# Reordering the transfers of an RMSNorm kernel and choosing the moment at which its stores are queued

## The chip, the cores and the metric

The kernel runs on one core of one Trainium2 chip. The metric is the device time of one execution in microseconds (us). The span in a profile is about 1.8 us shorter than the time (160.9 us against 162.69 us for the profiled run of the kernel before).

## The reference

```python
x: [16, 1024, 512] float32, gamma: ones(512), eps: 1e-5

def reference(x, gamma, eps):
    rms = np.sqrt(np.mean(x ** 2, axis=-1, keepdims=True) + eps)
    x_norm = x / rms * gamma
    return np.maximum(x_norm, 0).astype(np.float32)
```

That is 16,384 rows of 512 numbers: 33.55 MB in, 33.55 MB out, and very little arithmetic on each number.

## The kernel before

The rows are cut into eight chunks of 4 MB (128 partitions, 16 rows on each). There are six slots in SBUF, the on-chip memory, so chunks 6 and 7 reuse the slots of chunks 0 and 1. ACT (ScalarE) squares and sums, then takes the root; DVE (VectorE) multiplies by the reciprocal and gamma and clips at zero, in place. Both work in groups of eight rows, two groups to a chunk, sixteen in all. Every large transfer is issued from SP (SyncE) and so stands in one queue. This is the part that the change touches:

```python
    def store(i):
        nc.sync.dma_start(out=ov[i], in_=slot_ap(i)).then_inc(sem_slot[i % nslots], 16)
    ...
        for m, (i, a, r) in enumerate(loads):       # chunk 0 in two halves
            if i < nslots:
                load(m)
        nxt = nslots
        for i in range(nchunks):
            nc.sync.wait_ge(done, per * (i + 1))     # DVE has finished chunk i
            store(i)
            if i >= 1 and nxt < nchunks:
                nc.sync.wait_ge(sem_slot[nxt % nslots], 32)   # that slot's store has landed
                for m, (c, a, r) in enumerate(loads):
                    if c == nxt:
                        load(m)
                nxt += 1
    ...
        with nc.vector.Fori(0, ngroups) as gi:       # DVE, one group of eight rows
            ...
            for j in range(G):
                row = slots[:, bass.ds(base + j * d, d)]
                r = nc.vector.scalar_tensor_tensor(
                    out=row, in0=row, scalar=rstd[:, bass.ds(col + j, 1)], in1=gamma_sb,
                    op0=ALU.mult, op1=ALU.mult)
                if j == G - 1:
                    r.then_inc(sv, 1)
            ...
            nc.vector.tensor_scalar_max(out=blk, in0=blk, scalar1=0.0).then_inc(done, 1)
```

With L for a load, S for a store and the digit for the chunk, the queue holds L0 to L5, S0, S1, L6, S2, L7, S3 to S7.

## Time and profile before

| what | before | where it is read |
|---|---|---|
| time | 162.76 us, median of 3 (162.70 to 162.78) | timed runs |
| first packet starts, last ends | 1.96 us, 159.39 us | packet records of the trace |
| one transfer of 4 MB, first packet to the next one's first packet | 9.68 us, L5 alone 10.26 us | the same |
| DVE's last instruction ends | 146.43 us | timeline |

I call the time from a transfer's first packet to the first packet of the next a *stage*. If the queue never runs dry, the stages add up to the length of the stream, and the kernel's time is that length plus a fixed start and end. So the way to read this kernel is to list its stages and look for those that are longer than 9.68 us. I call such an excess a *lump*.

### The profile page before, as it was taken

How to read it: one execution, taken by the hardware profiler on the slowest of the kernel's cores; microseconds unless marked ns; L12 is line 12 of the kernel's file. 1: busy time of each engine (PE TensorE's matmuls, PEld its weight loads, DVE VectorE, ACT ScalarE, POOL GpSimd, SP SyncE). 2: the span in 40 equal slices, each digit the busy share in tenths (PEclk: the TensorE clock that was granted, in tenths of full speed). 3: DMA queues.
4: the chain of work that ended last, by engine and by line, in shares of the span. 5: the costliest groups of instructions: out<-in, count | busy, mean ns of one | idle time of the engine just before them, and what ended most of it. 6: DMA issues, size and time to landing. Idle time of an engine off the chain costs nothing. (4 is left out here: it accounts for less than half of the span.)

```text
span 160.9 us, 1006 instructions
## 1 busy us (share of the span) xinstructions
DVE 126.0 (78%) x164; ACT 86.3 (54%) x273; POOL 0.2 (0%) x4
## 2 busy tenths in 40 slices
DVE  1103989898989899999999999999999999994000
ACT  3088929889988988988900198503994000000000
POOL 0000000000000000000000000000000000000000
DMA  5999999999999998999999999999999999999993
GB/s 155 434 432 415 521 391 391 513 399 391 489 424 391 481 432 367 415 391 489 424 391 489 424 391 448 464 391 440 456 407 432 456 415 424 464 415 424 464 407 138
DMA packets 2456, 67.12 MB, mean 417 GB/s; under 512 B 276, under 2 KB 276, under 8 KB 280
## 3 DMA queue, kind: packets, MB, share of 16 engines
q1 hardware_dynamic: 2448, 67.11, 97.6%
q10 hardware_dynamic: 8, 0.01, 0.0%
HBM read 33.56 MB, written 33.55 MB: 417 GB/s over the span
## 5 line engine op out<-in xcount | busy, mean ns | idle before, releaser
L124 ACT ACTIVATE junk<-slots 128x512 f32 x128 | 74.5, 582 | 30.6 <-ACTq L120 30.3
L148 DVE SCALAR_TENSOR_TENSOR slots<-slots,rstd,gamma_sb 128x512 f32 x128 | 86.2, 747 | 4.8 <-DVEq L145 4.8
L155 DVE TENSOR_SCALAR slots<-slots x16 | 36.7, 2294 | 2.4 <-DVEq L154 0.2
L124 ACT ACTIVATION_READ_ACCUMULATOR junk<-slots x128 | 23.9, 187 | 0.0
L142 DVE RECIPROCAL rstd<-rms x16 | 3.1, 196 | 6.3 <-DVEq L138 6.3
L131 ACT ACTIVATE rms<-ss,eps_sb x16 | 4.8, 301 | 3.0 <-ACTq L130 3.0
L135 DVE LOAD_MASK_SELECT gamma_sb<-gseed x1 | 0.0, 14 | 5.8 <-DMA gseed<-in_gamma_dram 5.8
L116 ACT ACT_TABLE_LOAD x1 | 1.3, 1283 | 2.8 <-issue 2.8
L109 DVE MEMSET gseed<- 128x512 f32 x1 | 0.5, 485 | 1.1 <-SPq L90 1.1
L135 DVE STREAM_SHUFFLE gamma_sb<-gseed 128x512 f32<-128x512 f32 x1 | 0.7, 715 | 0.0
L180 POOL MEMSET const-bfloat16-1.0<- 128x1 bf16 x1 | 0.1, 103 | 0.0
L180 POOL MEMSET const-uint8-127<- 128x1 uint8 x1 | 0.1, 102 | 0.0
L180 POOL MEMSET const-float32-0.0<- 128x1 f32 x1 | 0.1, 100 | 0.2 <-issue 0.2
L180 POOL MEMSET const-float32-1.0<- 128x1 f32 x1 | 0.1, 99 | 0.0
L110 DVE MEMSET eps_sb<- 128x1 f32 x1 | 0.1, 59 | 0.0
## 6 DMA issues: line engine op xcount, KB each, us to landing
out_dram<-slots SPq DMA_DIRECT2D x8, 4096.0 KB, 31.3
slots<-in_x_dram SPq DMA_DIRECT2D x7, 4096.0 KB, 30.3
slots<-in_x_dram SPq DMA_DIRECT2D x2, 2048.0 KB, 9.6
gseed<-in_gamma_dram ACTq DMA_DIRECT2D x1, 8.0 KB
```

What stands on the lines that cost most here:

```text
L109: nc.vector.memset(gseed, 0.0).then_inc(sem_z, 1)
L110: nc.vector.memset(eps_sb, eps).then_inc(sem_z, 1)
L116: nc.scalar.preload_act_table(ACTF.Sqrt)
L124: a = nc.scalar.activation(out=junk[:, j, :], in_=slots[:, bass.ds(base + j * d, d)], func=ACTF.Square, accum_out=ss[:, bass.ds(col + j, 1)])
L131: nc.scalar.activation(out=rms[:, bass.ds(col, G)], in_=ss[:, bass.ds(col, G)], func=ACTF.Sqrt, bias=eps_sb, scale=inv_d).then_inc(sq, 1)
L135: nc.vector.stream_shuffle(gamma_sb, gseed, [0] * 32)
L142: nc.vector.reciprocal(out=rstd[:, bass.ds(col, G)], in_=rms[:, bass.ds(col, G)]).then_inc(sv, 1)
L148: r = nc.vector.scalar_tensor_tensor(out=row, in0=row, scalar=rstd[:, bass.ds(col + j, 1)], in1=gamma_sb, op0=ALU.mult, op1=ALU.mult)
L155: nc.vector.tensor_scalar_max(out=blk, in0=blk, scalar1=0.0).then_inc(done, 1)
L180: nc = _bacc.Bacc("TRN2", target_bir_lowering=False, num_devices=1)
```

## The change

L6 and L7 now stand together, which leaves two places where a store stands behind a load instead of three: S0 behind L5 and S2 behind L7. At both, SP holds the store back until DVE reaches a chosen row, so that it enters the queue when the last packets of that load are under way. The intent is to shorten the stream at these places. The stores' data are ready long before; no wait of another kind is removed.

```diff
     def store(i):
+        nc.sync.wait_ge(done, per * (i + 1))
         nc.sync.dma_start(out=ov[i], in_=slot_ap(i)).then_inc(sem_slot[i % nslots], 16)
...
-        nxt = nslots
-        for i in range(nchunks):
-            nc.sync.wait_ge(done, per * (i + 1))
+        nc.sync.wait_ge(tick3, 6)
+        store(0)
+        store(1)
+        for s in range(2):
+            nc.sync.wait_ge(sem_slot[s], 32)
+            load(7 + s)
+        nc.sync.wait_ge(tick1, 11)
+        for i in range(2, nchunks):
             store(i)
-            if i >= 1 and nxt < nchunks:
-                nc.sync.wait_ge(sem_slot[nxt % nslots], 32)
-                for m, (c, a, r) in enumerate(loads):
-                    if c == nxt:
-                        load(m)
-                nxt += 1
...
+                if j == 0:
+                    r.then_inc(tick1, 1)
+                if j == 2:
+                    r.then_inc(tick3, 1)
                 if j == G - 1:
                     r.then_inc(sv, 1)
```

(`load(7)` and `load(8)` are chunks 6 and 7, since chunk 0 has two loads.)

More of the change, by code (lines that the diff above doesn't have):

```diff
@@ L64 @@
     sq = tc.alloc_semaphore("sq")
+    tick1 = tc.alloc_semaphore("tick1")
+    tick3 = tc.alloc_semaphore("tick3")
     done = tc.alloc_semaphore("done")
```

## The prediction

> **What bounds the kernel now.** I read the page's DMA rows first, then the waits of the SP queue, then the busy time stage by stage, then the timelines of SP and of DVE. The page:
>
> ```profile
> span 160.9 us, 1006 instructions
> DVE 126.0 (78%) x164; ACT 86.3 (54%) x273; POOL 0.2 (0%) x4
> ...
> DMA  5999999999999998999999999999999999999993
> ...
> q1 hardware_dynamic: 2448, 67.11, 97.6%
> ```
>
> The 16 DMA engines are at nine tenths or more from the second slice to the last but one, and the one queue q1 holds 97.6% of them. DVE is busy for 78%, ACT for 54%. So the bound is the stream of 16 transfers of 4,194,304 bytes (8 loads, the first in halves, and 8 stores), all issued from SP in one order: L0 to L5, S0, S1, L6, S2, L7, S3 to S7. (L is a load, S a store, the digit the chunk.)
>
> From the packet records of the trace I took the first packet start of each transfer, 128 packets to each, and asked for the busy time of the windows between those edges. Columns: window, length, three engines, clock, DMA share, GB/s. The rows shown are L4, L5, S0, S1, L6, S2, L7, S3 and the last one, S7 with the end:
>
> ```profile
> 41.52:51.23 9.71, 9.26 (x13) 9.24 (x30) 0.00 (x0) 1.00 1.00 432
> 51.23:61.49 10.26, 9.81 (x14) 9.31 (x31) 0.00 (x0) 1.00 1.01 409
> 61.49:71.23 9.74, 9.14 (x12) 8.79 (x29) 0.00 (x0) 1.00 1.00 431
> 71.23:80.91 9.68, 8.94 (x13) 8.95 (x30) 0.00 (x0) 1.00 1.00 433
> 80.91:90.59 9.68, 9.23 (x13) 0.00 (x0) 0.00 (x0) 1.00 1.00 433
> 90.59:100.27 9.68, 9.23 (x13) 7.98 (x26) 0.00 (x0) 1.00 1.00 433
> 100.27:109.95 9.68, 9.23 (x13) 2.65 (x9) 0.00 (x0) 1.00 1.01 433
> 109.95:119.63 9.68, 9.08 (x13) 7.81 (x26) 0.00 (x0) 1.00 1.00 433
> ...
> 148.68:160.90 12.22, 0.00 (x0) 0.00 (x0) 0.00 (x0) 1.00 0.80 343
> ```
>
> A transfer takes 9.68 us from its first packet to the first packet of the next, load or store, whatever stands beside it. One is long: L5, 10.26 us at 409 GB/s. It stands ahead of the first store of all. In the packet records a 32 KB packet takes 1.213 us; the last packet of L5 on each engine starts at 59.80 to 60.18 us and takes 1.60 to 2.03 us. That is the only lump of the stream: **10.26 - 9.68 = 0.58 us**. The other two places where a store stands behind a load (L6 to S2, L7 to S3) and the two where a load stands behind a store (S1 to L6, S2 to L7) cost nothing: 9.68 us each.
>
> SP and the DVE work that the new waits hang on (start, length, engine, line):
>
> ```profile
> 31.07 16.83 SPq L87 DMA_DIRECT2D out_dram<-slots  x2
> 72.13 0.34 SPq L75 DMA_DIRECT2D slots<-in_x_dram  x1
> 72.51 0.73 SPq L87 DMA_DIRECT2D out_dram<-slots  x1
> 82.05 0.34 SPq L75 DMA_DIRECT2D slots<-in_x_dram  x1
> ...
> 55.69 0.20 DVE L142 RECIPROCAL rstd<-rms  x1
> ...
> 96.90 0.20 DVE L142 RECIPROCAL rstd<-rms  x1
> ...
> 144.14 2.29 DVE L155 TENSOR_SCALAR slots<-slots  x1
> ```
>
> S0 is issued at 31.07 us, 30 us before its first packet moves at 61.52. SP runs far ahead of the stream nearly everywhere, except at the very end: DVE finishes at 144.14 + 2.29 = 146.43, S7 is issued at 146.5, and its first packet moves at 148.71.
>
> **What the Trainium skill says.** "DMA: Bandwidth & Descriptors", section "Where 436 GB/s comes from", gives a ceiling of 435 GB/s for one core's DMA ports. The trace has 433 in every undisturbed stage, so no order of transfers can make a stage much shorter than 9.68 us: 67.11 MB at 435 GB/s would be 154.3 us (an estimate from that page), against 157.44 us that the stream takes now (first packet 1.98, last packet's end 159.42). The same page, "Latency and other measured facts", has about 0.6 us from an HWDGE issue to the first byte; here L0 is issued at 0.94 and its first packet starts at 1.98, that is 1.04 us, and I use the 1.04. "Perfetto Trace Analysis", in its part on the HWDGE instruction, says that the recorded DMA instruction leaves out the data movement; the trace agrees, 0.34 us of SP time for a 4 MB store that moves for 9.7 us. No page says what a change from reading to writing costs; the trace says zero in four of five places.
>
> **The change part by part.**
> (1) *S0's issue* moves from 31.07 us to the third row of the sixth DVE group (tick3 reaching 6). Group 6 has its reciprocal at 55.69, its first SCALAR_TENSOR_TENSOR at 56.18; eight of them take 5.39 us, so the spacing is (5.39 - 0.746) / 7 = 0.663 us, and the third ends at 56.18 + 2 x 0.663 + 0.746 = 58.25. SP answers a DVE semaphore in 146.5 - 146.43 = 0.07 us. First data can move at 58.25 + 0.07 + 1.04 = 59.36. Undisturbed, L5's last packets end at 59.80 + 1.21 = 61.01 and later. Margin 1.65 us: the queue does not run dry.
> (2) *L6 and L7 together, S2 behind L7.* L6 still waits for S0 to land (72.13) and L7 for S1 (82.05), as now; L6 moves at 80.94 and L7 takes the stage that S2 has now, 90.62 to 100.30. One change from load to store and one from store to load go; each cost 0. Saved: 0. L7 lands 9.68 us earlier, but DVE needs it only for its fifteenth group at 129.86: saved 0.
> (3) *S2's issue* waits for the first row of the eleventh group: 96.90 is its reciprocal, 97.39 its first row, so 97.39 + 0.746 = 98.14. First data at 98.14 + 0.07 + 1.04 = 99.25 against 100.30 when L7 is through, or 99.72 if the 0.58 us are gained. Margin 1.05 or 0.47 us: enough, but thin. S3 and S4 follow at once, their chunks being done at 80.5 and 97.0 us; S5 is done at 113.5 for a stage at 129.3, S6 at 129.9 for 139.0.
> (4) *Semaphore increments* on two of eight rows in each DVE group, with no instruction added (the compiled order has the same 29 DVE rows). An increment does not hold up the next instruction today: the TENSOR_SCALAR of line 155 carries one, and the next reciprocal starts 0.08 us before it ends (20.51 + 2.29 = 22.80 against 22.72). Cost: 0.
> (5) *The tail.* S7 can move at 146.5 + 1.04 = 147.54 at the earliest; its stage starts at 148.71 now, so up to 1.17 us of gain can be used before DVE sets the end.
>
> Sum: 162.76 - (0 to 0.58) + (0 to about 0.5 for thin margins). The only thing that can be won is the lump at L5; the intent, to queue a store late, aims at it.
>
> **The rivals.**
> *A: the lump comes of queueing S0 long ahead*; queued late it goes, and S2 behind L7 has none either. 162.76 - 0.58 = 162.2. For: it is the one place where six loads precede a store, and the change moves just this issue. Against: S2 and S3 are queued 18 and 27 us ahead of their data today and leave no lump.
> *B: the lump belongs to the first store of the run*, or to the end of a long run of loads, however it is queued. Then it stays: 162.7 to 162.8. For: the only lump is at the first store. Against: nothing in the trace.
> *C: a late issue leaves the engines dry.* If issue to first byte is 2 us under a full stream instead of 1.04, S2 starts at 100.2, just in time; at 2.5 us or more the gap is 0.4 us or more, and engines that finish early wait: 163.0 to 163.4. For: the thin margin. Against: S7, issued late today, starts 2.2 us after its issue with no gap at all.
> *D: the increments slow DVE*, say 0.08 us for each of 32: DVE ends at 149.0, S7 starts at 150.1, 1.4 us late, and the time is 164.1. Against: the overlap in (4).
>
> **Range and chances.** I give A 0.45, B 0.35, C 0.15, D 0.05. A's 162.2 and B's 162.75 weigh most; C and D pull up, a shrinking spread among the 16 engines (they end their last packets between 158.39 and 159.42) could pull A down by some tenths. I choose 162.3. The range adds about half a microsecond of run-to-run difference on each side: 161.5 to 163.1. Faster by over 2% would need 159.5 us, more than the whole loss of the stream (157.44 - 16 x 9.68 = 2.56 us, of which most is the start and the spread): 0.01. Slower by over 2% would need 166.0, which none of the rivals reaches: 0.02.
>
> **What would show it.** In the changed profile: SP issues S0 near 58.3 and S2 near 98.2; DVE still ends at 146.4; all inner stages at 9.68 us. A is right if L5's stage is 9.7 us and the last packet ends near 158.8; B if it is still 10.2; C if a gap stands ahead of S0 or S2; D if DVE's spacing of 0.663 us has grown. The prediction is wrong if a stage other than L5 changes its length, or if the time moves by more than 1.3 us.

## The result, and the profile after

The changed kernel takes 162.18 us (median of 6, 162.09 to 162.21) against 162.77 us in the same rounds (162.70 to 162.90). The ratio is 0.9962 with a 95% interval of 0.9949 to 0.9975: a small gain, clear of noise, far inside 2%. A ratio here is the mean time of one kernel's fast runs over that of the other's of the same rounds, with the profiled runs left out, so it is not quite the ratio of the medians quoted. Executions over 1.5% slower than the fastest of the same kernel are left out of the means.

The page of the changed kernel, the same rows as before:

```profile
span 160.4 us, 1008 instructions
DVE 126.0 (79%) x164; ACT 86.3 (54%) x273; POOL 0.2 (0%) x4
...
DMA  5999999999999999999999999999999999999993
...
q1 hardware_dynamic: 2448, 67.11, 97.6%
```

The span is shorter by half a microsecond. Of where, the page shows one digit: the sixteenth of its 4 us slices (60.3 to 64.4 us, where L5 gives way to S0) is 8 in the DMA row before and 9 after. No size can be read from that, and e11 below, with the same lump as before, has a 9 there. The stages show it. Busy time by stage in the changed kernel (columns: window, length, DVE, ACT, POOL, clock, DMA share, GB/s); the rows are L4, L5, S0, S1, L6, L7, S2, S3, and S7 with the end:

```profile
41.37:51.09 9.72, 9.27 (x13) 9.25 (x31) 0.00 (x0) 1.00 1.00 432
51.09:60.80 9.71, 9.26 (x13) 8.76 (x29) 0.00 (x0) 1.00 1.00 432
60.80:70.52 9.72, 9.12 (x13) 8.77 (x29) 0.00 (x0) 1.00 1.00 432
70.52:80.40 9.88, 9.43 (x11) 9.40 (x31) 0.00 (x0) 1.00 1.00 425
80.40:90.08 9.68, 8.94 (x14) 0.30 (x1) 0.00 (x0) 1.00 1.01 433
90.08:99.76 9.68, 9.23 (x13) 7.89 (x26) 0.00 (x0) 1.00 1.00 433
99.76:109.44 9.68, 9.23 (x13) 8.73 (x29) 0.00 (x0) 1.00 1.00 433
109.44:119.12 9.68, 9.23 (x13) 4.63 (x16) 0.00 (x0) 1.00 1.00 433
...
148.17:160.40 12.23, 0.00 (x0) 0.00 (x0) 0.00 (x0) 1.00 0.79 343
```

L5 went from 10.26 to 9.71 us; its last packet on each engine, 1.60 to 2.03 us long before, takes 1.21 to 1.30 us. A new, smaller lump stands at S1, ahead of L6: 9.88 us. The last packet ends at 158.84 us instead of 159.39. The difference of 0.55 us adds up from the stages: L5 -0.55, S1 +0.20, the first half of chunk 0 -0.15 (5.51 against 5.66 us), all the rest together -0.05. The start is not touched by the change: over these traces it scatters from 5.47 to 5.66 us (e10 left out, where a small store stands in it).

SP's and DVE's timelines of the changed kernel (start, length, engine, line):

```profile
58.35 0.82 SPq L90 DMA_DIRECT2D out_dram<-slots  x2
71.54 10.28 SPq L77 DMA_DIRECT2D slots<-in_x_dram  x2
98.23 48.62 SPq L90 DMA_DIRECT2D out_dram<-slots  x6
...
96.96 0.20 DVE L146 RECIPROCAL rstd<-rms  x1
...
144.20 2.29 DVE L163 TENSOR_SCALAR slots<-slots  x1
```

S0 is issued at 58.35 us instead of 31.07, S2 at 98.23 us instead of 72.51. DVE works as before and ends at 146.49 us. So the change acted where it was meant to. What remains is whether the lump went because of the moment of issue or because of the new order, and whether both waits are needed.

### The profile page after: what moved, and what is told of

Its sections match the earlier page's. It is cut to its first block, busy times and chain, and to the rows that moved or that the text cites. A ratio compares the mean times of both kernels' runs of the same rounds, so it can differ in the third digit from the quotient of the medians.

```text
span 160.4 us, 1008 instructions
## 1 busy us (share of the span) xinstructions
DVE 126.0 (79%) x164; ACT 86.3 (54%) x273; POOL 0.2 (0%) x4
```

## The experiments

**Theory A**: the lump comes of queueing a store long ahead behind a load. **Rivals**: the new order gains by itself; or the lump belongs to the first store, to a time or to a place in the run. Every kernel gave the right result. The lumps come from one profiled run of each kernel, the times from four or more.

### One part at a time: e1, e2, e3, e4

*e1* keeps the old order and adds only the wait ahead of S0 (the semaphores tick1 and tick3 are counted as in the change):

```diff
             nc.sync.wait_ge(done, per * (i + 1))
+            if i == 0:
+                nc.sync.wait_ge(tick3, 6)
             store(i)
```

> The kernel before with its old order of transfers, in which only the issue of the first store waits for the third row of DVE's sixth group (the two semaphores are counted as in the changed kernel). Theory A (the lump at the first store comes of queueing it some 30 us ahead): S0 issued at 58.3 us, the stage of the sixth load 9.7 us instead of 10.26, time 162.2 us, equal to the changed kernel. Theory B' (the new order, with fewer changes between loading and storing, is what gains): lump stays, 162.75 us.

Measured: 162.51 us against 162.95 us in the same rounds, ratio 0.9974 (0.9956 to 0.9992). Neither number was right. Busy time by stage, rows L5, S1, L6 (ahead of S2) and L7 (ahead of S3):

```profile
51.08:60.80 9.72, 9.27 (x13) 8.77 (x29) 0.00 (x0) 1.00 1.00 432
...
70.50:80.38 9.88, 9.43 (x11) 9.35 (x31) 0.00 (x0) 1.00 0.99 421
80.38:90.47 10.09, 9.35 (x15) 0.30 (x1) 0.00 (x0) 1.00 1.02 416
...
100.15:109.83 9.68, 9.23 (x13) 3.08 (x11) 0.00 (x0) 1.00 1.00 433
```

SP's issue of S2 in e1:

```profile
71.87 1.20 SPq L89 DMA_DIRECT2D out_dram<-slots  x1
```

The lump at L5 is gone, by the moment of issue alone. But another of 0.41 us now stands at L6, ahead of S2, which SP queued at 71.87 us, 18.6 us ahead of its first packet. In the kernel before, the same S2 was queued just as early and cost nothing. And L7, ahead of the equally early S3, has none. So the lump moved to the next early store.

*e2* is the changed kernel without its two waits, *e3* without the one ahead of S2, *e4* without the one ahead of S0:

```diff
-        nc.sync.wait_ge(tick3, 6)      # left out in e2 and e4
         store(0)
...
-        nc.sync.wait_ge(tick1, 11)     # left out in e2 and e3
```

> The changed kernel without its two new waits: loads 6 and 7 together, but every store queued as soon as its chunk is done. Theory A: S0 is issued at 31 us again, the sixth load's stage is about 10.26 us, time 162.75 us, equal to before. Theory B': no lump or a smaller one, 162.2 us.

> The changed kernel without the wait ahead of S2; the wait ahead of S0 stays. Theory A in its strong form (any store queued long ahead behind a load makes a lump): S2, queued at 82 us behind L7, lengthens L7's stage by about 0.6 us, 162.75 us. Theory A in its weak form (only behind the long run of loads at the start): no lump anywhere, 162.2 us. The kernel before speaks for the weak form: S2 and S3 were queued early there and left no lump.

> The changed kernel without the wait ahead of S0; the wait ahead of S2 stays. Theory A: the lump of 0.58 us at the sixth load is back, 162.75 us. Theory B': 162.2 us.

| kernel | S0 queued, lump at L5 | S2 queued, lump ahead of it | time | ratio to before |
|---|---|---|---|---|
| e2, order only | 30.95 us, 0.78 us | 82.36 us, none | 162.86 us | 0.9998 (0.9981 to 1.0014) |
| e3, S0 late | 58.33 us, 0.07 us | 81.90 us, 0.43 us | 162.53 us | 0.9974 (0.9957 to 0.9990) |
| e4, S2 late | 30.98 us, 0.83 us | 98.08 us, none | 162.62 us | 0.9980 (0.9963 to 0.9997) |

The rows that matter, L5 ahead of S0 in e2 and L7 ahead of S2 in e3:

```profile
51.07:61.53 10.46, 9.93 (x14) 9.51 (x32) 0.00 (x0) 1.00 1.00 401
...
90.06:100.17 10.11, 9.66 (x14) 8.05 (x26) 0.00 (x0) 1.00 1.02 415
```

The order alone gains nothing (e2), which refutes the rival that the new order gains by itself. With S0 late and S2 early the lump falls at S2 (e3), as in e1. In e2 the early S2 costs nothing, because S0 has had the lump before it: e2 and e3 differ in the wait ahead of S0 alone.

The edges of a stage are those of the first engine to get there. Averaged over the 16 engines, the lump is 0.71 us before, 0.63 us in e1 and 0.54 us in e3, so it moved nearly whole. The engines' last packets end at 158.70 us on average before, at 158.73, 158.69 and 158.76 us in e1, e3 and e4 (for the last two in their slowest runs, see below), and at 158.13 us in the changed kernel. In these profiles, then, one wait without the other gains nothing on average, and both together gain. e4's time fits less well: by its lump of 0.83 us it should equal before, yet it lies between the two. Its profiled run was the slowest of four (162.88 us; the others 162.51 to 162.63), and so was that of e3 (162.96 us; the others 162.40 to 162.62), so the lump need not have its full size in every execution. That was not looked into further. The number expected for e3, 162.75 or 162.2 us, did not come either.

### Only once, wherever it stands: e6

S0 moved up behind L3, everything queued as early as it can be:

```diff
             if i < nslots:
                 load(m)
+            if i == 3:
+                nc.sync.wait_ge(done, per)
+                store(0)
...
-            store(i)
+            if i > 0:
+                store(i)
```

> The kernel before with S0 moved up behind L3, all stores queued as soon as their chunks are done: L0 to L3, S0, L4, L5, S1, L6, S2, L7, S3 to S7. Theory once (only the first store that is queued ahead behind a load makes a lump, wherever it stands): L3's stage is 10.2 to 10.5 us, and those of L5, L6 and L7 are 9.7; 162.8 us. Rival each (every long run of loads before a store makes one): lumps at L3 and L5, 163.2 us or more. Rival place (the lump belongs to about 60 us of the run or to six loads in a row): L3 9.7 us.

Measured: 163.22 us against 163.00 us, ratio 1.0025 (1.0004 to 1.0047). Busy time by stage in e6, rows L3 (ahead of S0), L5 (ahead of S1), L6 (ahead of S2), L7 (ahead of S3):

```profile
31.77:42.23 10.46, 10.01 (x14) 9.51 (x31) 0.00 (x0) 1.00 1.01 401
...
61.59:71.27 9.68, 9.09 (x12) 7.89 (x26) 0.00 (x0) 1.00 1.00 433
...
80.95:90.63 9.68, 9.22 (x13) 4.63 (x16) 0.00 (x0) 1.00 1.01 433
...
100.31:110.00 9.69, 9.24 (x13) 2.92 (x11) 0.00 (x0) 1.00 1.01 433
```

The lump follows S0 to L3 (0.78 us). The time came out at the number of rival each (163.2 us), not at the 162.8 us of theory once; but the second lump of that rival, at L5, is not there. The three stores behind it, all queued early, have none, L5's with two loads ahead of it included. So it is neither the place, nor the 60 us, nor six loads in a row. It strikes the first early store, once.

### How late is late enough: e7, e11

Both are the changed kernel with another wait ahead of S0; in e11 it is the end of DVE's fifth group:

```diff
-        nc.sync.wait_ge(tick3, 6)
+        nc.sync.wait_ge(tick3, 5)      # e7
+        nc.sync.wait_ge(done, 5)       # e11
```

> The changed kernel with S0 waiting for the third row of DVE's fifth group instead of the sixth: issued at about 50.1 us, a microsecond before L5's first packet moves, 10 to 11 us before its own. If what counts is to be queued within the load's last few microseconds, as the intent of the change has it: lump of about 0.6 us at L5, 162.7 us. If 20 to 30 us ahead are needed for a lump: no lump, 162.2 us.

> The changed kernel with S0 waiting for DVE's fifth group to be done: issued at about 55.9 us, 5 us ahead of its first packet, with L5 half through. Between 58.3 us (no lump) and 50.05 us (lump of 0.6 us). If a store must not be queued before the load ahead of it has begun to move: no lump, 162.2 us. If only the last 3 us are harmless: lump of 0.4 to 0.6 us, 162.6 to 162.8 us.

Busy time of L5's stage in e7:

```profile
51.07:61.39 10.32, 9.87 (x14) 9.37 (x31) 0.00 (x0) 1.00 1.01 406
```

and in e11:

```profile
51.18:61.53 10.35, 9.90 (x14) 9.40 (x31) 0.00 (x0) 1.00 1.02 408
```

| kernel | S0 issued | ahead of its first packet | lump at L5 | time | ratio to before |
|---|---|---|---|---|---|
| before | 31.07 us | 30.4 us | 0.58 us | 162.77 us | 1 |
| e7 | 50.05 us | 11.3 us | 0.64 us | 162.86 us | 1.0001 (0.9984 to 1.0017) |
| e11 | 55.76 us | 5.8 us | 0.67 us | 162.89 us | 0.9992 (0.9969 to 1.0015) |
| after | 58.35 us | 2.5 us | 0.03 us | 162.18 us | 0.9962 (0.9949 to 0.9975) |

The first 25 us of delay buy nothing, the last 2.6 us buy everything. It is not enough that the load has begun to move: in e11 L5 was nearly half through. The limit lies between 5.8 and 2.5 us, or between about five and two packets of 1.213 us. It may not be sharp: in the profile of e8 (below), which leaves the wait ahead of S0 as it is, S0 was issued at 58.19 us, 2.8 us ahead, and L5 has 0.12 us. In e7, e11 and the changed kernel S1 is issued right behind S0; the two were not moved apart.

### Too late: e8

The changed kernel with S2 held until the third row of DVE's eleventh group instead of the first:

```diff
-        nc.sync.wait_ge(tick1, 11)
+        nc.sync.wait_ge(tick3, 11)
```

> The changed kernel with S2 waiting for the third row of DVE's eleventh group instead of the first: issued at about 99.55 us, 0.2 us before L7's packets end on the first engine. With 1.04 us from issue to first packet, as at the start of the run, S2 starts at 100.6 instead of 99.76, and the kernel takes 0.8 us longer: 163.0 us. If the latency is 2 us under a full stream (rival C of the prediction): 1.8 us longer, 164.0 us.

SP's issue of S2 in e8:

```profile
99.40 47.30 SPq L90 DMA_DIRECT2D out_dram<-slots  x6
```

Busy time of L7's stage and of the last one with the end:

```profile
90.10:100.24 10.14, 9.69 (x14) 8.42 (x28) 0.00 (x0) 1.00 0.97 417
...
148.94:160.40 11.46, 0.00 (x0) 0.00 (x0) 0.00 (x0) 1.00 0.84 363
```

S2's first packet moves 100.24 - 99.40 = 0.84 us after its issue, so on the engine that was through first the queue was dry for about 10.14 - 9.68 = 0.46 us; the DMA share of the stage falls to 0.97. It is no lump: L7's last packets take 1.21 to 1.22 us. The loss is less than the 0.8 us expected, and far from the 2 us of the rival. The time hardly shows it: 162.29 us, ratio 0.9967 (0.9950 to 0.9984). The last stage is shorter, since the engines now end close together. In the changed kernel the 16 engines end their last packets at 158.13 us on average and 158.84 us at the latest; in e8 at 158.72 and 158.91 us. The average came 0.59 us later, the latest engine only 0.07 us, and the latest sets the end. The packet records show where they draw together: in e8 the engines end L7 between 99.81 and 100.23 us and all start S2 between 100.24 and 100.39 us, after the same issue, so those that were through early waited longest (0.30 us on average). In the changed kernel, without a gap, they start S2 over 0.61 us. That this gap is what keeps them close to the end was not tested.

### Paying the lump with a small store: e9, e10

The kernel before with an extra store of 64 KB, queued early behind L1 (e9) or behind the first half of chunk 0 (e10). S7 waits for it, then writes over it.

```diff
             if i < nslots:
                 load(m)
+            if m == 2:                 # e9; m == 0 in e10
+                nc.sync.wait_ge(sem_q, 1)
+                nc.sync.dma_start(out=ov[nchunks - 1][:, 0, 0:128], in_=zrow).then_inc(sem_t, 16)
...
+            if i == nchunks - 1:
+                nc.sync.wait_ge(sem_t, 16)
```

> The kernel before with one extra store of 64 KB (512 zero bytes for each of 128 rows that S7 writes over later; the result stays right), queued at about 3 us behind L1, so some 19 us ahead of its turn. All else as before. Theory once, whatever the size: the lump of about 0.6 us falls at L1 and none at L5; 162.8 us plus a few tenths for the extra packets. Theory that the lump needs a large store behind it: none at L1, 0.58 us at L5, the time of before plus a few tenths. If both have one: not once for a run.

> The same with the small store behind the first half of chunk 0, where the engines are still starting. Theory once, whatever the size, and the lump can lie beside the start: L5 9.7 us and no lump elsewhere, 162.3 us, as good as the changed kernel without any of its waits. If the lump is paid in full at L0: 162.8 us. If size matters: L5 stays at 10.3 us.

Measured: 162.88 us (ratio 0.9998, 0.9976 to 1.0021) and 163.04 us (1.0003, 0.9979 to 1.0026). L1's and L5's stages in e9:

```profile
12.41:22.29 9.88, 7.36 (x10) 6.94 (x23) 0.00 (x0) 1.00 0.99 426
51.33:61.59 10.26, 9.81 (x14) 9.31 (x31) 0.00 (x0) 1.00 1.00 409
```

In e9, L1's stage is 9.88 us, and the extra 0.20 us is what the small store itself takes (eight packets of 0.027 us on each engine, 0.22 us). The lump at L5 is 0.58 us in both. So an early store of 64 KB neither has a lump nor uses it up; no size between that and 4 MB was tried.

### The lump that is left: e5, and the changed kernel again: e12

*e5* holds L6 back as well, until DVE's eighth group has done its sixth row:

```diff
         store(1)
+        nc.sync.wait_ge(tick6, 8)
         for s in range(2):
...
+                if j == 5:
+                    r.then_inc(tick6, 1)
```

> The changed kernel, in which the issue of L6 too waits, for the sixth row of DVE's eighth group (76.8 us by the changed kernel's timeline), so that it is queued some 3.4 us before S1 ends instead of 9 us. The changed kernel has one lump left, 0.2 us at S1 to L6 (a stage of 9.88 us). If any first transfer of the other direction that is queued long ahead makes a lump, it goes: all inner stages 9.68 to 9.72 us, 162.0 us, 0.2 below the changed kernel. If the lump belongs to the change from storing to loading as such, 162.2 us.

> The changed kernel once more, beside the three others on the same chip. Its lumps should be where they were: none at L5 and L7, 0.2 us at S1; 162.2 us, ratio to before 0.996.

e5 issued L6 at 76.98 us, 3.2 us ahead of its first packet, and S1's stage is 9.68 us: that lump is gone. But L6 and S2 have 9.75 us each, the last packet ends at 158.81 us, much as in the changed kernel (158.84), and the time is 162.22 us, ratio 0.9960 (0.9946 to 0.9973): no gain over the change. In e12, the changed kernel on that chip, S1's stage was 9.76 us instead of 9.88, so this lump is small and not steady. It stands in every profile with S0 late and L6 early (0.08 us in e12, 0.09 in e8, 0.20 to 0.21 in the changed kernel, e1 and e3) and in none of the eight with S0 early, where S1's stage is 9.68 us. e12 took 162.34 us, ratio 0.9964 (0.9942 to 0.9987): the result repeats. No version here beat the changed kernel.

## Why the prediction was right

It said 162.3 us, within 161.5 and 163.1; 162.18 came out. By its own steps:

- **The bound and the lump.** Right: the 0.58 us at L5 was what the change could win, and the stage lost 0.55 us. e11 and e7 show that the moment of issue does it: the same kernel with an earlier S0 has the lump again. It is not all that there is to be won: the latest engine ends 0.71 us behind the average in the changed kernel, and 0.20 us in e8. One line was misread: the DMA row is not at nine from the second slice to the last but one, since its sixteenth digit, at the lump, is 8.
- **Step 1, S0's issue.** Predicted near 58.3, measured 58.35 us, with no gap before its first packet. (SP answers DVE in 0.03 us, not 0.07: S7's issue is at 146.46 us, which the prediction read from a rounded 146.5.)
- **Step 2, "Each cost 0. Saved: 0".** This step failed. It read from the trace of before that S2 and S3, queued 18 and 27 us ahead, leave no lump, so queueing a store early behind L6 or L7 was free, and the wait ahead of S2 could only do harm. It is free only after S0 has had the lump; once S0 is late, the early S2 has it (0.41 us in e1, 0.43 us in e3). The wait ahead of S2 therefore counts: without it (e3) L7's stage is 10.11 us, with it 9.68 us. In time the difference is not clear of noise: the changed kernel's ratio is 0.9962 and 0.9964, e1's and e3's 0.9974, and these intervals overlap. The order alone did save 0 (e2); whether it is needed at all, with S2 and S3 held back in the old order, no run tests. That the sum still came out right is luck in this term: the change happens to hold back both stores, and the prediction had no gain in the second wait.
- **Step 3, the thin margin at S2.** No gap came. From issue to first packet it takes 0.84 us beside a full stream (e8) instead of the 1.04 us taken from the start, so the margin was larger. Rival C fell with that. (Rival C's sum was mixed: it measured S2 against 100.30 us, but with the lump gained L7 is through at 99.72, measured 99.76 us, and its 2 us would already have left a gap of 0.5 us.)
- **Steps 4 and 5.** DVE ended at 146.49 us against 146.43, so the increments cost nothing that counts, and rival D fell. S7 starts at 148.17 us, still after its issue.
- **Rival A against B.** A held: L5's stage is 9.71 us and the last packet ends at 158.84 us, where the prediction asked for 9.7 and 158.8. B (the lump belongs to the first store, however it is queued) is refuted by the changed kernel itself, whose L5 stage is 9.71 us. The point held against A, that S2 and S3 leave no lump, has its explanation in e1, e3 and e6.
- **Not foreseen**: the small lump at S1, 0.20 us in one profile of the changed kernel and 0.08 us in the other. "All inner stages at 9.68 us" was wrong there, and a stage other than L5 that changes its length is one of the prediction's own signs of being wrong.

Left open: what the DMA engines do in the lump, why it strikes once and only with a large store, and why its size ranges from 0.41 to 0.83 us.

## What to carry to other kernels

In a kernel bound by its transfer stream, list the stages from first packet to first packet; a loss of half a microsecond, which in 4 us slices is one digit at most, stands out there. A cost that strikes only once makes its later occasions look free, so before concluding from them, remove the first one and look where the cost goes. Holding back a transfer until the last two packets ahead of it can be worth trying, but it needs the time from issue to first packet measured beside a full stream, and here the whole gain was 0.4%.

## What the Trainium skill lacked or had wrong

- "DMA: Bandwidth & Descriptors", section "Rules for kernel authors", advises to issue a DMA early and wait on its semaphore late. It has no word on a queue that is never dry, where the first large store queued 5.8 to 30.4 us ahead behind a load cost 0.58 to 0.67 us (before, e7, e11), and one queued 2.5 us ahead cost 0.03 us.
- The same page, "Latency and other measured facts", gives about 0.6 us from an HWDGE issue to the first byte. Here it is 1.02 us at the start (0.94 to 1.96 us) and 0.84 us beside a full stream (e8), from the recorded start of the issue to the recorded start of the first packet.
- No page says what a change between loading and storing costs. Here a stage ahead of such a change takes 9.68 us, as any other does, except for the lump told of above and one of about 0.2 us at S1, ahead of L6 (after, e1, e3).
- No page says how far apart the 16 engines get within one queue fed from SP: in the changed kernel their first packets lie 0.61 us apart at S2 and 0.99 us at S7, and one of them ends its last packet 0.71 us later than the average and sets the end.
